# Projections over pairs of 256-token blocks, with 512-column matmuls, in a hybrid GLA and SSD encoder

## The chip, the cores and the metric

The kernel runs on one core of a Trainium2 chip. Its time is the device time of one execution in microseconds (us). One execution is profiled; the durations below are from that one, and the times of the runs stand beside it.

## What is computed

One encoder layer over 2048 prompt tokens and 256 sample tokens, model width 1024, all in float32:

```python
u = _rmsnorm(h, norm_g)
proj = u @ w_in            # q, k, v, z_gla, lr, z_ssd, xbc, dt
...
o = (_gla_direction(q, k, v, la[:, :, 0], False)
     + _flip(_gla_direction(_flip(q), _flip(k), _flip(v), _flip(la[:, :, 1]), True)))
o = _rmsnorm(o, gla_onorm_g).reshape(bt, L, GLA_VAL)
o = o * jax.nn.silu(z_gla.astype(f32))
xbc = jax.nn.silu(_centred_dwconv(xbc, conv_w) + conv_b).astype(f32)
...
y = (_ssd_direction(xs, dt[:, :, 0], A[0], bm, cm, False)
     + _flip(_ssd_direction(_flip(xs), _flip(dt[:, :, 1]), A[1], _flip(bm), _flip(cm), True)))
y = y + d_skip.astype(f32).reshape(SSD_GROUPS, SSD_HPG)[..., None] * xs
y = _rmsnorm(y.reshape(bt, L, SSD_WIDTH) * jax.nn.silu(z_ssd.astype(f32)), ssd_norm_g)
h = h + jnp.concatenate([o, y], axis=-1) @ w_out
h = h + jax.nn.sigmoid(h @ w_ple_gate) * _rmsnorm(p @ w_ple_proj, ple_norm_g)
```

GLA (gated linear attention, 4 heads) and SSD (Mamba-2, 4 groups) are chunked scans, once forward and once backward over the tokens.

## The kernel before

Tokens lie in 9 blocks of 256 (8 of the prompt, 1 of the sample). Each float32 factor of a large product is split into a high and a low part, and the product is three matmuls: high by high (L183), high by low (L184), low by high (L185), made in `mm3`. A projection of one block to 256 columns, a *group*, is so 8 x 2 x 3 = 48 matmuls with 256 streamed columns.

Eight passes go over the blocks, s0 to s7: the even ones a GLA head (blocks 0 to 8), the odd ones an SSD group (blocks 8 to 0). In a pass each block has three groups: `pq` and `pv` (q/k and v) or `pxa` and `pxb` (x, and B with C), and `pz`, the gate of the pass before. Split inputs u are read from DRAM (`uD`, `load_u`) for every block again, in four pieces, two of them early (`Operand`) and two when the third group begins (`rest`).

The first direction of a block (`gla_first`, `ssd_first`) is put into `queue` and is emitted behind a later group by `behind`, up to QMAX behind. The second direction (`second`) needs all blocks of the pass, so it is done in the next pass, behind the group after its gate (`carry`). Until then its running sum y1 and the decayed q (or C), qd, stay in SBUF, 10 buffers each, and only the chunk states U go to DRAM (`put_U`). A GLA block needs its decay first: `gla_decay` makes log decays (`log_decay`: a small matmul into the tile pg, then ScalarE and POOL), cumulative sums on VectorE (L450) and two exponentials, and `gla_qk` multiplies q and k by them while reading PSUM. An SSD block needs a convolution (`ssd_conv`, L604 on VectorE), a B/C product that VectorE masks (cbm, L648) and decay matrices (G, L686 and L687).

After the passes `output` makes three sweeps over the blocks with the output weights (foa, fob, fpg).

A scheduler of the framework orders the instructions of each engine from the program's order and its own cost model. PSUM has 8 banks: 4 with the tag pj (groups and pg), 3 with p1, 1 with p2. All DMAs are issued in one order from SP's queue, and one that waits holds back those behind it.

## Time and profile before

| | |
|---|---|
| time, median of 3 runs | 2574.34 us (2572.82 to 2578.37) |
| the profiled execution | 2581.07 us, its span 2579.3 us |
| TensorE's mean granted clock | 0.974 of full speed |
| TensorE busy | 2437.3 us, 94% |
| VectorE busy | 1744.1 us, 68% |
| ScalarE busy | 1227.3 us, 48% |
| POOL busy | 630.9 us, 24% |
| data moved by SP's queue | 411.66 MB |

Busy times come from one execution; a share is a mean over the whole span. In the trace the first sweep goes to 241 us, the seven later passes to 1756 us, foa to 2037, fob to 2270, and fpg to the end. Tile names are those of the program: `s3b1fpb` is pass 3, block 1, first direction, tile pb; `s4b1d...` is the decay of pass 4's block 1; `pq`, `pv`, `pz`, `pxa` and `pxb` are groups. PE is TensorE, DVE VectorE, ACT ScalarE.

### The profile page before, as it was taken

The page shows a single profiled execution, that of the slowest core. Times are in us where ns is not written, and L with a number is a line of the kernel's source. Part 1 is how long each engine was busy: PE and PEld are TensorE (multiplying, and loading weights), DVE is VectorE, ACT ScalarE, POOL GpSimd, SP SyncE. Part 2 cuts the span into 40 slices and gives each one's busy share as a digit, 9 for nine tenths or more (in the row PEclk, how much of TensorE's full clock was granted, in tenths as well). Part 3 has the DMA queues.
Part 4 walks back from the last instruction along what each step waited for, and adds up shares of the span by engine and source line. Part 5 has one row for each costly group of instructions (what it writes and reads, how often), then busy time and mean ns, then how long its engine had stood idle before and what let it go on. Part 6 is the DMA issues. An engine that isn't in the chain of part 4 may idle for free. (4 is left out here: it accounts for less than half of the span.)

```text
span 2579.3 us, 51675 instructions
## 1 busy us (share of the span) xinstructions
PE 2437.3 (94%) x19736; PEld 2377.1 (92%) x19736; DVE 1744.1 (68%) x4012; ACT 1227.3 (48%) x2468; POOL 630.9 (24%) x649
## 2 busy tenths in 40 slices
PE   7999999899999989999989999998989999998897
PEld 7999999799999979999989999997988889998897
DVE  8886799864579984468997456899623333456665
ACT  5565456644445654445565443565311222355555
POOL 3231000043200023320003330001434432255552
PEclk9999999899999989999999999998999999999998
DMA  6456456544755644465564446555755565512221
GB/s 234 162 173 200 145 184 202 155 138 146 216 169 175 194 135 157 158 201 168 170 206 142 145 150 193 169 162 176 226 163 169 188 207 173 157 51 72 74 75 59
DMA packets 296170, 415.06 MB, mean 161 GB/s; under 512 B 33596, under 2 KB 140904, under 8 KB 295912
## 3 DMA queue, kind: packets, MB, share of 16 engines
q1 hardware_dynamic: 295912, 411.66, 50.7%
q8 instruction: 157, 2.57, 0.4%
q14 instruction: 101, 0.83, 0.1%
HBM read 319.21 MB, written 92.35 MB: 160 GB/s over the span
## 5 line engine op out<-in xcount | busy, mean ns | idle before, releaser
L183 PE MATMUL pz<-u_h,wh_n 128*128 128x256 f32 x896 | 255.6, 285 | 0.0
L185 PE MATMUL pz<-u_h,wl_n 128*128 128x256 f32 x896 | 255.3, 285 | 0.0
L184 PE MATMUL pz<-u_l,wh_n 128*128 128x256 f32 x896 | 255.1, 285 | 0.0
L184 PEld LDWEIGHTS pz<-u_l,wh_n 128*128 128x128 f32 x896 | 171.0, 191 | 0.7 <-issue 0.7
L185 PEld LDWEIGHTS pz<-u_h,wl_n 128*128 128x128 f32 x896 | 170.9, 191 | 0.6 <-issue 0.5
L183 PEld LDWEIGHTS pz<-u_h,wh_n 128*128 128x128 f32 x896 | 171.0, 191 | 0.2
L183 PE MATMUL pxb<-u_h,wh_n 128*128 128x256 f32 x512 | 147.5, 288 | 0.0
L184 PE MATMUL pxa<-u_l,wh_n 128*128 128x256 f32 x512 | 147.2, 287 | 0.0
L183 PE MATMUL pxa<-u_h,wh_n 128*128 128x256 f32 x512 | 146.8, 287 | 0.0
L184 PE MATMUL pxb<-u_l,wh_n 128*128 128x256 f32 x512 | 146.2, 286 | 0.0
L185 PE MATMUL pxb<-u_h,wl_n 128*128 128x256 f32 x512 | 145.8, 285 | 0.0
L185 PE MATMUL pxa<-u_h,wl_n 128*128 128x256 f32 x512 | 145.3, 284 | 0.0
L183 PE MATMUL pq<-u_h,wh_n 128*128 128x256 f32 x384 | 113.4, 295 | 1.6 <-DMA u_h<-uD 1.2
L183 PE MATMUL pv<-wh_n,u_h 128*128 128x256 f32 x384 | 110.9, 289 | 0.7 <-DVE s4b1dm L508 0.2
L185 PE MATMUL pv<-wh_n,u_l 128*128 128x256 f32 x384 | 111.5, 290 | 0.0
L185 PE MATMUL pq<-u_h,wl_n 128*128 128x256 f32 x384 | 111.4, 290 | 0.0
L184 PE MATMUL pq<-u_l,wh_n 128*128 128x256 f32 x384 | 111.2, 290 | 0.0
L184 PE MATMUL pv<-wl_n,u_h 128*128 128x256 f32 x384 | 108.7, 283 | 0.0
L183 PEld LDWEIGHTS pxa<-u_h,wh_n 128*128 128x128 f32 x512 | 97.9, 191 | 1.6 <-issue 1.4
L183 PEld LDWEIGHTS pxb<-u_h,wh_n 128*128 128x128 f32 x512 | 97.9, 191 | 0.7 <-issue 0.7
L184 PEld LDWEIGHTS pxa<-u_l,wh_n 128*128 128x128 f32 x512 | 97.9, 191 | 0.5 <-issue 0.2
L184 PEld LDWEIGHTS pxb<-u_l,wh_n 128*128 128x128 f32 x512 | 97.8, 191 | 0.5 <-issue 0.5
(5981 smaller groups left out, 9561.1 us busy)
## 6 DMA issues: line engine op xcount, KB each, us to landing
u_h<-uD SPq DMA_DIRECT2D x224, 256.0 KB
u_l<-uD SPq DMA_DIRECT2D x224, 256.0 KB
wr_n<-wsec SPq DMA_DIRECT2D x48, 512.0 KB
fx<-xT SPq DMA_DIRECT2D x36, 256.0 KB
h1D<-fx SPq DMA_DIRECT2D x36, 256.0 KB
fh<-h1D SPq DMA_DIRECT2D x36, 256.0 KB
hD<-fh SPq DMA_DIRECT2D x36, 256.0 KB
wr_oa<-wlast SPq DMA_DIRECT2D x8, 512.0 KB
```

The costliest lines, as they stand in the source:

```text
L183: te.matmul(outs, lhsT=lh, rhs=rh, start=start and k == ks[0], stop=False, skip_group_check=True)
L184: te.matmul(outs, lhsT=lh, rhs=rl, start=False, stop=False, skip_group_check=True)
L185: te.matmul(outs, lhsT=ll, rhs=rh, start=False, stop=stop and k == ks[-1], skip_group_check=True)
```

## The change

The seven later passes go over pairs of blocks, `SBS = [(0, 1), (2, 3), (4, 5), (6, 7), (8,)]`, with the last block alone. `proj_pair` makes a group for both blocks of a pair: where tokens are streamed (q/k, x, B/C, z) a matmul has 512 columns, and where tokens are the weights (v) it keeps 256. The 72 pair groups with 512 columns are 28 gates, 28 first groups and 16 SSD second ones, 48 matmuls each. The four pj banks become two tiles of two banks (`bank_pair`); the first sweep and the output sweeps use halves of them. A group is emitted in two halves, with `carried` and `behind` after each. u lies in DRAM by pairs and is loaded in eight pieces (high and low part each 256 KB) with nine buffers each, one piece ahead and seven in `rest`. y1 and qd of every block but a pass's last now go to DRAM too (`keep`) and come back with U in `second_loads`; this makes room in SBUF, and fewer buffers of y1, qd and mx are kept. Raw weights come in quarters. The tile pg of `log_decay` moves from pj to p1.

```diff
 QMAX = 2
+UW = 2 * T
 UK = 2
-UBUFS = 6
+RAWS = 3
+UBUFS = 9
...
+    banks = {"p1": 3, "p2": 1}
+    halves = []
+
+    def bank_pair(name):
+
+        return pp.tile([P, 2, 512], F32, name=name, tag="pj", bufs=2)

     def bank(tag, shape, name):
-        return pp.tile(shape, F32, name=name, tag=tag, bufs=banks[tag])
-
-
-
-    uD = [dram.tile([KT // UK, 2, P, UK, T], F32, name=f"uD{b}") for b in range(NB)]
+        if tag != "pj":
+            return pp.tile(shape, F32, name=name, tag=tag, bufs=banks[tag])
+        if not halves:
+            t = bank_pair(name)
+            halves.extend((t[:, 1], t[:, 0]))
+        h = halves.pop()
+        return h[:, 0:shape[1]] if len(shape) == 2 else h.rearrange("p (f t) -> p f t", f=shape[1])
...
+    uD = [dram.tile([KT, 2, P, T * len(sb)], F32, name=f"uD{n}") for n, sb in enumerate(SBS)]
...
+    yD = [[dram.tile([P, 2, T], F32, name=f"yD{b}_{q}") for q in range(2)] for b in range(NB)]
+    qD = [[dram.tile([P, T], F32, name=f"qD{b}_{q}") for q in range(2)] for b in range(NB)]
...
-    def load_raw(src, tag, kh):
-        raw = upool.tile([P, 4, T], F32, name=f"wr_{tag}_{kh}", tag="uraw", bufs=2)
-        sy.dma_start(raw, src[kh])
+    def load_raw(src, tag, n):
+        raw = upool.tile([P, 2, T], F32, name=f"wr_{tag}_{n}", tag="uraw", bufs=RAWS)
+        sy.dma_start(raw, src[n // 2, :, 2 * (n % 2):2 * (n % 2) + 2])
         return raw
...
+    def proj_pair(w, u, nb, name, token_major):
+        ps = bank_pair(name)
+        flat = ps.rearrange("p f t -> p (f t)").rearrange("p (c t) -> p c t", c=4)
+        def half(h):
+            for k in range(h * KT // 2, (h + 1) * KT // 2):
+                wk, uk = [t[:, k % 4] for t in w[k // 4]], [t[:, 0] for t in u[k]]
+                if token_major:
+                    for c in range(2 * nb):
+                        mm3(flat[:, c], lambda _: [t[:, c * C:(c + 1) * C] for t in uk], lambda _: wk, [k],
+                            k == 0 and c % 2 == 0, k == KT - 1)
+                else:
+                    for f in range(2):
+                        mm3(ps[:, f, :nb * T], lambda _: [t[:, f * P:(f + 1) * P] for t in wk],
+                            lambda _: [t[:, :nb * T] for t in uk], [k], k == 0, k == KT - 1)
+        part = lambda j: flat[:, 2 * j:2 * j + 2] if token_major else ps[:, :, j * T:(j + 1) * T]
+        return half, part
...
-        bufs = {"t4k": 2, "dk": 6, "tm": 2, "zo": 4, "eb": 2, "mx": 7, "q1": 3, "lr": 2, "y1": 10, "qd": 10, "ac": 12,
-                "Us": 1, "Ul": 2, "S1": 2, "S2": 2, "xr": 2, "xc": 2, "ad": 3, "wg": 1, "tot": 3, "hl": 1}
+        bufs = {"t4k": 2, "dk": 6, "tm": 2, "zo": 4, "eb": 2, "mx": 6, "q1": 3, "lr": 2, "y1": 4, "qd": 5, "ac": 12,
+                "yl": 2, "ql": 2, "Us": 1, "Ul": 2, "S1": 2, "S2": 2, "xr": 5, "xc": 2, "ad": 3, "wg": 1, "tot": 3, "hl": 1}
...
-            pg = bank("pj", [P, 2, T], nm + "pg")
+            pg = bank("p1", [P, 2, T], nm + "pg")
...
+        def keep(s, b, U):

             if b == s.order[-1]:
                 s.U = U
             else:
                 sy.dma_start(UD[b][s.i % 2], U)
+                sy.dma_start(yD[b][s.i % 2], s.y1.pop(b).rearrange("p c f i -> p (c f i)").rearrange("p (f t) -> p f t", f=2))
+                sy.dma_start(qD[b][s.i % 2], s.qd.pop(b))
             s.done.add(b)
...
+            if b == s.order[-1]:
+                U, y1, q = s.U, s.y1.pop(b), s.qd.pop(b)
+            else:
+                U, y1, q = tmp("Ul", [P, 2, T], nm + "U"), tmp("yl", [P, 2, 2, C], nm + "y"), tmp("ql", [P, T], nm + "q")
                 sy.dma_start(U, UD[b][s.i % 2])
-            return U, ebc(1 - s.d1, s.h, b, nm + "e2") if s.kind == "s" else None
+                sy.dma_start(q, qD[b][s.i % 2])
+                sy.dma_start(y1.rearrange("p c f i -> p (c f i)").rearrange("p (f t) -> p f t", f=2), yD[b][s.i % 2])
+            return U, y1, q, ebc(1 - s.d1, s.h, b, nm + "e2") if s.kind == "s" else None
...
+            sbs = list(dict.fromkeys(sb_of(b) for b in s.order))
+            for n, sb in enumerate(sbs):
+                last = n == len(sbs) - 1
+                blocks = [b for b in s.order if b in SBS[sb]]
+                if not last:
+                    u2 = load_u(sbs[n + 1], f"u{i}_{sbs[n + 1]}")
                 elif nxt is not None:
+                    u2 = load_u(sb_of(nxt.order[0]), f"u{i}n")
                 else:
                     u2 = gla_mix(NB - 1, "fa8")
+                steps = need(i) if n == 0 else need(i)[1:] + need(i)[:1]
                 for g, (wn, what) in enumerate(steps):
+                    w = get_w(wn)
+                    if g == 2:
                         u2.rest()
+                    half, part_of = proj_pair(w, u, len(blocks), f"p{what}{i}_{sb}", s.kind == "g" and what == "b")
+                    for h in range(2):
+                        late = len(queue)
+                        half(h)
+                        carried()
+                        if s.kind == "g" and what == "a" and h == 0:
+                            for b in blocks[1:]:
+                                gla_decay(s, b, wg, lrs.pop(0))
+                        if h == 0:
                             behind(late)
+                    for b in blocks:
+                        ps = part_of(b - SBS[sb][0])
+                        if what == "z":
+                            zz = gate_z(ps, f"z{i}_{b}")
+                            carry.append(lambda a=(prev, b, zz): second(*a))
+                        elif s.kind == "g" and what == "a":
+                            gla_qk(s, b, ps)
+                        elif s.kind == "g":
+                            v = tmp("mx", [P, 2, T], f"v{i}_{b}")
+                            sc.activation(v, ps, AF.Copy)
+                            hl = [tmp("xr", [P, 2, T], f"v{i}_{b}s{q}", F32R) for q in range(2)]
+                            split(v, *hl, sc, ve)
+                            queue.append(lambda a=(s, b, v, tuple(hl)): gla_first(*a))
                         else:
+                            ssd_raw(s, b, 0 if what == "a" else 1, ps)
+                    behind(late)
+                    if g == 1 and s.kind == "g" and not last:
+                        ahead = [b for b in s.order if sb_of(b) == sbs[n + 1]]
+                        lrs = [load_lr(b, f"s{i}b{b}lr") for b in ahead]
+                        gla_decay(s, ahead[0], wg, lrs.pop(0))
                     elif g == 0 and s.kind == "s" and last and nxt:
+                        ahead = [b for b in nxt.order if sb_of(b) == sb_of(nxt.order[0])]
+                        lrs = [load_lr(b, f"s{i + 1}b{b}lr") for b in ahead]
+                        gla_decay(nxt, ahead[0], wg, lrs.pop(0))
```

The order of instructions shows three places. First TensorE, where pass 3 (SSD) ends and pass 4 (GLA) begins, before the change. Each row is the first of a run for that tile (`pq4_1` is block 1's group in pass 4; s3b1fpb and s3b0fpb are the B/C products of the last two SSD blocks, fpy a product with the decay matrices, s4b1dpg the decay matmul of block 1):

```order
L183 MATMUL pz4_0_12015<-u3n_h0_11574,wh_n11_0_10536 128x256
...
L183 MATMUL pq4_0_12090<-u3n_h0_11574,wh_n12_0_11734 128x256
...
L477 MATMUL s4b1dpg_12193<-s4b1lr_11709,s4wg_10554 128x256
...
L183 MATMUL pv4_0_12219<-wh_n13_0_11869,u3n_h0_11574 128x256
...
L183 MATMUL pq4_1_12352<-u4_1_h0_12003,wh_n12_0_11734 128x256
...
L641 MATMUL s3b1fpb_11935<-s3b1qd_11659,s3b1c0xc_11675 128x128 x2
...
L183 MATMUL pv4_1_12494<-wh_n13_0_11869,u4_1_h0_12003 128x256
...
L183 MATMUL pz4_1_12602<-u4_1_h0_12003,wh_n11_0_10536 128x256
...
L641 MATMUL s3b0fpb_12272<-s3b0qd_11680,s3b0c0xc_11696 128x128 x2
...
L183 MATMUL pq4_2_12684<-u4_2_h0_12340,wh_n12_0_11734 128x256
...
L708 MATMUL s3b0fpy_12401<-s3b0fG1_12306,s3b0fxt_12284 64x128 x4
...
L183 MATMUL pv4_2_12808<-wh_n13_0_11869,u4_2_h0_12340 128x256
```

After the change (`pa4_0` is q/k of blocks 0 and 1 together, `pb4_0` their v, `pa4_1` q/k of blocks 2 and 3):

```order
L203 MATMUL pz4_0_10821<-u3n_h0_10088,wh_n11_0_9512 128x512
...
L203 MATMUL pa4_0_10928<-u3n_h0_10088,wh_n12_0_10310 128x512
...
L679 MATMUL s3b2fpb_10542<-s3b2qd_10211,s3b2c0xc_10227 128x128 x2
...
L679 MATMUL s3b1fpb_10737<-s3b1qd_10237,s3b1c0xc_10253 128x128 x2
...
L203 MATMUL pb4_0_11269<-wh_n13_0_10608,u3n_h0_10088 128x256
...
L679 MATMUL s3b0fpb_10993<-s3b0qd_10258,s3b0c0xc_10274 128x128 x2
...
L746 MATMUL s3b0fpy_11059<-s3b0fG1_11027,s3b0fxt_11005 64x128 x4
...
L517 MATMUL s4b1dpg_11123<-s4b1lr_10287,s4wg_9540 128x256
...
L568 MATMUL s4b0fpa_11442<-s4b0qq1_11201,s4b0dm_10291 128x128
...
L203 MATMUL pa4_1_11396<-u4_1_h0_10803,wh_n12_0_10310 128x512
```

What moved: before, the groups pz4_0 to pq4_2, seven of them, stand ahead of SSD block 0's fpy product, and block 1's decay matmul stands far ahead of it. After, three pairs (pz4_0, pa4_0, pb4_0) do, and the decay matmul of block 1 stands behind it and ahead of pa4_1.

The same place on VectorE, before, behind SSD block 0's masked product (L450 and L452 are the cumulative sums of a decay, fmin a running minimum, ac copies of chunk decays):

```order
L506 SCALAR_TENSOR_TENSOR s4b1qq1_12464<-pq4_1_12352,s4b1dE_12211 128x256
L686 SCALAR_TENSOR_TENSOR s3b0fG1_12306<-s3b0fcbm_12282,s3b0ftm_12286,s3b0fG1_12306 128x128
L450 SCALAR_TENSOR_TENSOR s4b2de_12578<-s4b2dm_12579,bounds_220 128x128
L452 SCALAR_TENSOR_TENSOR s4b2de_12578<-s4b2dm_12579,bounds_220 128x128
...
L686 SCALAR_TENSOR_TENSOR s3b0fG1_12306<-s3b0fcbm_12282,s3b0ftm_12286,s3b0fG1_12306 128x128 x3
L491 TENSOR_TENSOR fmin_223<-fmin_223,s4b2de_12578 128x2
L515 COPY s4b2ac_12761<-s4b2dE_12595 128x1
...
L687 TENSOR_TENSOR s3b0fG1_12306<-s3b0fG1_12306,s3b0ffb1_12295 128x512
...
L506 SCALAR_TENSOR_TENSOR s4b2qq1_12762<-pq4_2_12684,s4b2dE_12595 128x256
...
L687 TENSOR_TENSOR s3b0fG0_12327<-s3b0fG0_12327,s3b0ffb0_12316 128x512
```

After the change, from the same decay matrix G1 on:

```order
L724 SCALAR_TENSOR_TENSOR s3b0fG1_11027<-s3b0fcbm_11003,s3b0ftm_11007,s3b0fG1_11027 128x128 x4
L724 SCALAR_TENSOR_TENSOR s3b0fG0_11048<-s3b0fcbm_11003,s3b0ftm_11007,s3b0fG0_11048 128x128 x4
L725 TENSOR_TENSOR s3b0fG1_11027<-s3b0fG1_11027,s3b0ffb1_11016 128x512
...
L725 TENSOR_TENSOR s3b0fG0_11048<-s3b0fG0_11048,s3b0ffb0_11037 128x512
...
L760 TENSOR_TENSOR s3b0y1_10257<-s3b0fpy_11059,s3b0y1_10257 128x512
L519 TENSOR_SCALAR s4b1dm_11125<-s4b1dpg_11123,bg_279 128x256
L817 TENSOR_TENSOR s3b0lo_11109<-s3b0lpf_11108,s3b0le2_11096 128x2x128
L519 TENSOR_SCALAR s4b1dm_11125<-s4b1dpg_11123,bg_279 128x256
L817 TENSOR_TENSOR s3b1lo_11178<-s3b1lpf_11177,s3b1le2_11105 128x2x128
L490 SCALAR_TENSOR_TENSOR s4b1de_11124<-s4b1dm_11125,bounds_252 128x128
```

What moved: the sums of the decays of s4's blocks 1 and 2 no longer stand among pass 3's last decay matrices; those of block 1 (s4b1dm, L519) stand behind the last sums of SSD block 0.

Last SP's queue, the u loads for block 6 in pass 4 before, with what each waits for:

```order
L176 DMA u4_6_h0_13536<-uD6_75 128x512 [waits DMAHW5_49,PE_49]
L176 DMA u4_6_l0_13537<-uD6_75 128x512 [waits DMAHW6_49]
L176 DMA u4_6_l1_13539<-uD6_75 128x512 [waits DMAHW7_49,PE_49]
L176 DMA u4_6_h1_13538<-uD6_75 128x512 [waits DMAHW0_49,PE_49]
L740 DMA s3b6lU_13881<-UD6_1_172 128x512 [waits DMAHW1_49,Pool_49]
L731 DMA UD4_0_167<-s4b4fU_13640 128x512 [waits DMAHW2_49,Activation_49]
L627 DMA s3b6le2_13883<-ebD6_111 64x2x256 [waits DMAHW3_49,DVE_49]
L627 DMA s3b6le2_13883<-ebD6_111 64x2x256 [waits DMAHW4_49]
L782 DMA mixD4_118<-z4_4zz_13503 128x512 [waits DMAHW5_49,Pool_49]
L787 DMA sqD4_136<-s3b4lo_13603 128x256 [waits DMAHW6_49,Pool_49]
L176 DMA u4_6_l2_13541<-uD6_75 128x512 [waits DMAHW7_49,PE_49]
L176 DMA u4_6_h2_13540<-uD6_75 128x512 [waits DMAHW0_49,PE_49]
```

And those of pair 3 (blocks 6 and 7) after the change:

```order
L196 DMA u4_3_l0_11850<-uD3_72 128x512 [waits DMAHW0_49,PE_49]
L196 DMA u4_3_h0_11849<-uD3_72 128x512 [waits DMAHW1_49,PE_49]
L770 DMA UD2_0_195<-s4b2fU_11816 128x512 [waits DMAHW2_49,Activation_49]
L771 DMA yD2_0_159<-s4b2y1_11482 128x512 [waits DMAHW3_49,Activation_49]
L783 DMA s3b4lq_11985<-qD4_1_182 128x256 [waits DMAHW4_49,PE_49]
...
L826 DMA mixD2_112<-z4_2zz_11809 128x512 [waits DMAHW0_49,Pool_49]
...
L771 DMA yD3_0_161<-s4b3y1_11498 128x512 [waits DMAHW0_49,Activation_49]
...
L831 DMA sqD3_131<-s3b3lo_11993 128x256 [waits DMAHW5_49,Pool_49]
L196 DMA u4_3_l1_11852<-uD3_72 128x512 [waits DMAHW6_49,PE_49]
L196 DMA u4_3_h1_11851<-uD3_72 128x512 [waits DMAHW7_49,PE_49]
L196 DMA u4_3_l2_11854<-uD3_72 128x512 [waits DMAHW0_49,PE_49]
L196 DMA u4_3_h2_11853<-uD3_72 128x512 [waits DMAHW1_49,PE_49]
```

What moved: between the first loads and the rest stood six other transfers, and now stand some twenty; an eighth of the data (two transfers of sixteen) comes early, where half of it did, and the others wait for TensorE one by one.

## Rows read from the trace of the kernel before

**Rows 1.** Page, part 1: busy time, share of the span and count by engine

```profile
span 2579.3 us, 51675 instructions
PE 2437.3 (94%) x19736; PEld 2377.1 (92%) x19736; DVE 1744.1 (68%) x4012; ACT 1227.3 (48%) x2468; POOL 630.9 (24%) x649
```

**Rows 2.** Windows over one SSD and GLA cycle; first row names the columns

```profile
core 0: us, PE busy (x) PEld busy (x) DVE busy (x) ACT busy (x) POOL busy (x), PEclk, DMA share, GB/s
772.00:953.00 181.00, 170.22 (x1364) 161.62 (x1362) 165.12 (x450) 107.39 (x247) 4.99 (x5) 0.96 0.55 173
953.00:1125.00 172.00, 170.55 (x1441) 169.58 (x1442) 94.65 (x206) 75.09 (x121) 66.00 (x86) 1.00 0.50 163
```

**Rows 3.** Timeline of TensorE in a group: start us, us, engine, line, tiles

```profile
600.38 0.28 PE L183 MATMUL pv<-wh_n,u_h 128*128 128x256 f32 x1
...
601.10 0.28 PE L183 MATMUL pv<-wh_n,u_h 128*128 128x256 f32 x1
```

**Rows 4.** Timeline of TensorE, weights of 128 and 64 columns in turn

```profile
97.96 0.28 PE L332 MATMUL g3ps<-p3u_h,wsm 128*128 128x256 f32 x1
98.07 0.28 PE L334 MATMUL g3ps<-p3u_l,wsm 128*64 128x256 f32 x1
...
98.66 0.28 PE L332 MATMUL g3ps<-p3u_h,wsm 128*128 128x256 f32 x1
```

**Rows 5.** Timeline of TensorE, a run of four plain float32 matmuls

```profile
721.64 1.02 PE L705 MATMUL s3b8fpu<-s3b8fxh,s3b8fbt 128*128 128x256 f32 x4
```

**Rows 6.** Timeline of VectorE: a convolution, first mask, last decay matrix

```profile
734.76 1.40 DVE L604 SCALAR_TENSOR_TENSOR s3b7c0cc<-xr,cw,s3b7c0cc 128x256 f32<-128x256 f32 x3
...
778.68 0.68 DVE L648 TENSOR_TENSOR s3b6fcbm<-s3b6fpb,mask 128x512 f32<-128x512 f32 x1
...
953.84 0.74 DVE L687 TENSOR_TENSOR s3b0fG<-s3b0fG,s3b0ffb 128x512 f32<-128x512 f32 x1
```

**Rows 7.** Timeline of TensorE: the bounds of the stretches

```profile
689.92 0.36 PE L183 MATMUL pxa<-u2n_h,wh_n 128*128 128x256 f32 x1
...
957.51 0.38 PE L183 MATMUL pv<-wh_n,u_h 128*128 128x256 f32 x1 [0.15 <-DVE s4b1dm L508]
...
1124.66 0.36 PE L183 MATMUL pxa<-u4n_h,wh_n 128*128 128x256 f32 x1
```

**Rows 8.** VectorE's prices: timeline rows, and a group by line (count, busy, mean ns)

```profile
930.20 0.42 DVE L450 TENSOR_TENSOR_SCAN s4b1de<-s4b1dm,bounds 128x128 f32<-128x128 f32 x1 [1.19 <-POOL s4b1dm L482]
...
933.15 0.48 DVE L479 TENSOR_SCALAR s4b2dm<-s4b2dpg,bg 128x256 f32<-128x256 f32 x1 [0.26 <-ACT s4b2de L478]
...
945.34 0.42 DVE L506 SCALAR_TENSOR_TENSOR s4b1qq<-pq,s4b1dE 128x256 f32<-128x256 f32 x1
...
948.06 0.15 DVE L515 COPY s4b2ac<-s4b2dE 128x1 f32<-128x1 f32 x1
...
956.78 0.67 DVE L508 TENSOR_TENSOR s4b1dm<-pq,s4b1dm 128x512 f32<-128x512 f32 x1
...
958.58 2.87 DVE L513 TENSOR_SCALAR s4b1qkh<-s4b1dm,s4b1dE 128x128 f32<-128x128 f32 x4
...
L147 DVE TENSOR_TENSOR wl_n<-wr_n,wh_n 128x1024 fp32r<-128x1024 f32 x46 | 56.7, 1235 | 26.5 <-ACT wh_n L144 26.3
```

**Rows 9.** Timeline of a decay: its matmul, ScalarE, then POOL

```profile
998.37 0.29 PE L477 MATMUL s4b4dpg<-s4b4lr,s4wg 96*128 96x256 f32 x1
...
1001.15 0.63 ACT L481 ACTIVATE s4b4de<-s4b4de 128x512 f32<-128x512 f32 x1
...
1001.86 1.30 POOL L482 TENSOR_TENSOR s4b4dm<-s4b4dm,s4b4de 128x512 f32<-128x512 f32 x1 [8.70 <-ACT s4b4de L481]
```

**Rows 10.** A window with a burst of transfers, columns as above

```profile
1046.00:1050.00 4.00, 4.00 (x37) 4.00 (x36) 0.43 (x1) 3.96 (x5) 1.30 (x1) 1.00 0.98 344
```

**Rows 11.** Waits of SP's queue: us in total, times, longest us

```profile
SPq L176 <- PE pz L185: 192.3, 164, 4.3
...
SPq L740 <- POOL s5b6lS L443: 8.9, 1, 8.9
```

More of the change, by code (lines that the diff above doesn't have):

```diff
@@ L167, in rest @@
             if self.piece:
-                for n in range(2, KT // UK):
+                for n in range(self.ahead, len(self.parts)):
                     self.piece(n, *self.parts[n])
@@ L388, in prep_dt2, with carried @@
             sy.dma_start(tmD[b], tm)
[L392 to L397 removed]
+        queue, carry, summed, sums_due = [], [], set(), []
+        def carried(ps=None):
+            if carry:
+                carry.pop(0)()
             return ps
         def behind(n):
[L402 removed]
+            if n and queue:
                 queue.pop(0)()
@@ L826, in gla_rstd @@
         def gla_rstd(bs, nm):
+            assert all((b, h) in summed for b in bs for h in range(NH))
             rc = tmp("lr", [NH * len(bs), T], nm + "rc")
@@ L866, in hybrid @@
+        for i, s in enumerate(secs[1:], 1):
+            prev, nxt = secs[i - 1], secs[i + 1] if i < 7 else None
             for n, _ in need(i):
                 get_w(n)
-            for n, b in enumerate(s.order):
-                last = n == NB - 1
-                if i == 0 and b == 0:
-                    pass
-                elif i == 0 and not last:
-                    sums = prep_sums(b + 1, xs)
-                elif not last:
-                    b2 = s.order[n + 1]
-                    if s.kind == "g" and n + 2 < NB:
-                        lrs.append(load_lr(s.order[n + 2], f"s{i}b{s.order[n + 2]}lr"))
-                    u2 = load_u(b2, f"u{i}_{b2}")
+            sbs = list(dict.fromkeys(sb_of(b) for b in s.order))
[4 more added lines that the diff above has]
+                    u2 = load_u(sbs[n + 1], f"u{i}_{sbs[n + 1]}")
@@ L880, in hybrid @@
                 elif nxt is not None:
-                    u2 = load_u(nxt.order[0], f"u{i}n")
+                    u2 = load_u(sb_of(nxt.order[0]), f"u{i}n")
                 else:
                     u2 = gla_mix(NB - 1, "fa8")
-                steps = need(i) if n == 0 or i == 0 else need(i)[1:] + need(i)[:1]
+                steps = need(i) if n == 0 else need(i)[1:] + need(i)[:1]
                 for g, (wn, what) in enumerate(steps):
-                    w, late = get_w(wn), len(queue)
-                    if g == 2 and (i or last):
+                    w = get_w(wn)
+                    if g == 2:
```

225 lines of the change are left out of this document (110 added, 115 removed).

## The prediction, made before the changed kernel was run

> **What bounds the kernel now.** I read the page's busy shares first. TensorE is busy 94% of a span of 2579.3 us and VectorE 68% [rows 1], so a change that makes matmuls cheaper looks as if it were worth its full saving. But a mean hides stages, and the windows by stage show two [rows 2]. One SSD pass and the GLA pass behind it (s3 and s4) make up 435 us, and three such cycles follow each other. In the second half of the SSD pass and the start of the GLA pass (772 to 953 us) VectorE is busy 165.12 of 181 us, while TensorE's granted clock falls to 0.96: TensorE waits there. From 953 us on it is the other way round: VectorE 94.65 of 172 us, TensorE 170.55 at clock 1.00. So the cycle is a VectorE stretch, up to the decay matrices of SSD block 0 (953.84 + 0.74 = 954.6 us [rows 6]), and then a TensorE stretch, from the value projection of block 2 (957.51) to the first matmul of the next SSD pass (1124.66) [rows 7]. The reader is to see that a saving on TensorE counts in full only in the second stretch, and that the first stretch gets shorter only if VectorE starts earlier or has less to do.
>
> **Price of a wide matmul.** A 256-column matmul in a row of its kind follows the one before after 120 ns: six steps in 0.72 us [rows 3]. Where weights of 128 and of 64 columns alternate it is 0.70 / 6 = 117 ns [rows 4]. At 2.4 GHz and one column a cycle, 256 columns would be 106.7 ns, so 13.3 ns come on top with 128 weight columns and 10.0 with a mean of 96: the extra goes with the weights, not with the streamed columns. A 512-column matmul should therefore take 213.3 + 13.3 = 226.7 ns, which I take, and the pair saves 13.3 ns. The bounds: four plain fp32 matmuls over 256 columns took 1.02 us with some 0.38 us of the last one's latency in it, (1.02 - 0.38) / 3 = 213, or 216 ns with rounding [rows 5]; that is 512 cycles at 2.4 GHz or a little over, so they are the nearest row to 512 columns. Twice 120 is 240 ns. The 3,456 wide matmuls (72 groups of 48) would save 46 us if all lay on the path. They don't.
>
> The Trainium skill's page "TensorE: Matmul & The Clock Gate" (section "Back-to-back issue gap") gives N / 2.4 + 2.5 ns for an isolated matmul: 216 at 512 columns, 109 at 256. The second figure disagrees with the 120 ns of this trace, and by the page alone a pair would save only 3 ns, an estimate of 9 us over all wide matmuls.
>
> **The VectorE stretch.** It begins for s3 with its first matmul at 689.92 us [rows 7]. In the new order, block 6's B/C product, which VectorE masks at 778.68 before [rows 6], stands behind two groups of the lone block (48 x 0.12 = 5.8 us each), six wide groups (48 x 0.2267 = 10.9 us each), 15 matmuls of a seventh (3.4 us) and small ones that I put at 6.2 us: 86.6 us, so the mask comes at 776.5, 2.1 us sooner. From there to block 0's last decay matrix I count VectorE's instructions in both orders. Out of the stretch go s4's own (8 scans and 2 drains of 0.42, 4 clamps of 0.48, a split of 0.67, 4 products of 2.87 / 4 = 0.72, a dozen copies and minima of 0.1 to 0.15 [rows 8]: 11.3 us), because only block 0 of s4, not blocks 1 and 2, stands ahead of the last SSD block; and 17 of s3's own steps, mostly convolution steps at 1.40 / 3 = 0.47 [rows 6], which are done before the mask (7.6 us at a mean of 0.45). Into it come 2.5 us of s2's second directions and gates, and 0.9 us for splitting weights in 12 pieces of 0.69 instead of 6 of 1.235 [rows 8], less 0.3 us of edge copies. The balance is -15.8 us of work, at the stretch's busy share 165.12 / 181 = 0.91 [rows 2] -17.4 us of time. Its end moves to 954.6 - 2.1 - 17.4 = 935.1 us. Bounds: nothing at all, if the operations that leave were filling gaps, and -20 us.
>
> **What is paid for that.** The GLA groups that used to cover the end of the VectorE stretch were seven; now six equivalents (three pairs) are issued, and the seventh, the q/k pair of blocks 2 and 3 (pa4_1), stands behind the decay matmul of block 1, which itself stands behind block 0's SSD product. It cannot start sooner for lack of PSUM: one of the two bank pairs holds block 1's q and k until they have been multiplied by their decay, and the other holds the values of pb4_0. From the decay matmul at 998.37 to the end of POOL's 1.30 us at 1003.16 it took 4.8 us [rows 9]; then come 4 scans (1.7 us) and the drains (two of 0.42 and one of 0.67, 1.5 us [rows 8]), and between them two exponentials of 0.63 [rows 9]: 9.3, taken as 9 us, and TensorE has little else in that time. So the TensorE stretch starts at 935.1 + 0.5 (last product) + 9 = 944.6 us instead of 957.5. The bounds of this wait are 0 (block 1's decay is done in the shadow of block 0's last steps) and 9.3 us.
>
> **The TensorE stretch.** Before it is 167.2 us [rows 7]: 21 groups of 5.76 make 121.0, and 46.2 are small matmuls and waits, which I leave. After it holds 288 wide matmuls (65.3 us) and 480 of 256 columns (57.6 us), 122.9 + 46.2 = 169.1 us: one group more. It ends at 1113.7, 11.0 us before 1124.66.
>
> **The sum.** Three cycles give -33 us. The last SSD pass hands over to the output sweep, with no decay to wait for: -2.1 from the mask and -7.6 / 0.91 = -8.4 from the steps done earlier, of which I count -8 in all, since the output sweep waits for transfers of its own as well. Everything else I put at nothing: the first sweep keeps its 256-column matmuls, and its stores in shorter runs, the halved weight loads and the 393 KB that 64 blocks now write to DRAM and read back (64 x 0.393 x 2 = 50 MB) go through queues that moved 163 to 173 GB/s [rows 2] where 344 GB/s were reached [rows 10]; that is the cover, and where it fails is the slow rival below. 2581.07 - 41 = 2540 for the profiled execution, which was 6.7 us above the median of its runs, so 2574.3 - 41 = **2533 us**.
>
> **The token loads.** They are the cover that could break. Each piece now waits for the piece that it overwrites, and seven of eight are issued in the third group of the pair before. Each k is a piece of two times 256 KB: at 344 GB/s [rows 10] 1.5 us, against 1.36 us of matmuls on it. The last of the seven lands some 14 us after that group starts, and is read at about 23.5: a slack of 9.5 us. Between the first and the second piece the queue now holds some twenty other transfers, of which those that store s4's results wait for ScalarE, VectorE and POOL. The longest wait that the queue had on such a store or load was 8.9 us, its longest on TensorE's release of a piece 4.3 us, 192.3 us in 164 times [rows 11].
>
> **The rivals.**
> - Dearer matmuls: 240 ns. The mask comes 4.0 us later and the TensorE stretch is 288 x 0.0133 = 3.8 us longer: 7.8 per cycle, 27 in all with the last pass, **2560 us**. For it speaks only that nothing streamed 512 fp32r columns before; against it, the row with 64 weight columns.
> - Cheaper matmuls, and a warmer clock: at 216 ns the two stretches gain 3.2 and 3.1 us, 22 in all, **2511 us**. For it: the plain fp32 row [rows 5]. The Trainium skill's page "TensorE: Matmul & The Clock Gate" gives the same 216 ns at 512 columns. If TensorE also stops waiting, the 0.04 of clock that is missing over 181 us [rows 2] is worth up to 7 us per cycle: **2490 us**.
> - Slower, the lookahead: if VectorE's end stays at 954.6, the 9.5 us of the decay and the longer TensorE stretch (1.9 us), less the 2.9 that lay between 954.6 and 957.5, cost 8.5 us per cycle: **2599 us**. It decides where the VectorE stretch shortens by less than 8.5 of my 19.5 us. For it: one group less of cover, and block 1's decay behind the last SSD product. Against it: the counted operations, on an engine that is 91% busy.
> - Slower, the loads: a wait of 8.9 us on a store ahead of the pieces, with 4.3 behind it, passes the slack by 3.7 us; at 35 pair starts that is 130 us, **2660 us**. It decides at 41 / 35 = 1.2 us per pair. Against it: such a wait occurred once.
> - No change: the two ends of the VectorE stretch's bounds cancel the rest, **2574 us**.
>
> **How the numbers follow.** The forecast, a gain of 20 to 60 us with 226.7 or so per wide matmul, has 48%; the cheaper matmul with or without the clock 13%; the dearer one or a gain under 20 us 12%; no change 5%; the lookahead 13%; the loads 9%. A measurement of this kernel can tell 0.2% (5 us) from nothing. Faster is 48 + 13 + 12 = 0.73, same 0.05, slower 0.22. The range leaves out the late loads and the far end of the gains: 2490 to 2600 us. The forecast's own is 2514 to 2554.
>
> **What the profile after would show.** Consecutive 512-column matmuls 227 ns apart; 213 to 216 or 240 name the first two rivals. VectorE nearly never idle in the SSD pass, and block 0's last decay matrix done 245 us behind the pass's first matmul, instead of 954.6 - 689.9 = 265. A gap on TensorE ahead of pa4_1 that ends on s4b1's exponentials, some 9 us long: without it that term is wrong, and with it and VectorE's end unmoved it is the lookahead rival. TensorE's waits on transfers of uD at the start of pairs near nothing; several us each are the load rival. A cycle, first matmul of one SSD pass to that of the next, of 424 us instead of 435. The forecast is wrong at its root if VectorE is not what ends the SSD pass once blocks come in pairs.

## The result, and the profile after

The changed kernel takes 2709.94 us (median of 4 runs, 2703.92 to 2716.99) against 2574.2: the ratio is 1.053, with an interval of 1.051 to 1.055. It was forecast at 2533, with a range that ended at 2600. The profiled execution took 2709.12 us. Its page, part 1:

```profile
span 2707.5 us, 45656 instructions
PE 2451.8 (91%) x16280; PEld 2231.1 (82%) x16280; DVE 1752.4 (65%) x4084; ACT 1236.7 (46%) x2542; POOL 629.1 (23%) x651
```

There are 3,456 matmuls fewer, as planned, and yet TensorE's busy time is a little longer than in [rows 1]; its mean granted clock is 0.953 in this execution, where it was 0.974. The first question is where the 128 us of span arose. The first matmuls of pass 1's x group, of foa and of fpg cut both traces into four stages; this table gives their lengths in us, here with the kernels that the experiments below turn on:

| kernel | first sweep | seven passes | foa, fob | last sweep |
|---|---|---|---|---|
| before | 246.9 | 1509.3 | 513.8 | 309.4 |
| after | 283.0 | 1564.4 | 514.4 | 345.7 |
| e1, before with pg in p1 | 254.2 | 1520.5 | 509.9 | 305.6 |
| e2, before with bank pairs | 269.9 | 1565.6 | 515.3 | 313.8 |
| e9, after with single banks, pg in pj | 258.1 | 1536.9 | 510.7 | 289.7 |
| e15, e9 without pairs of blocks | 259.7 | 1542.7 | 501.7 | 290.2 |
| e17, before with DRAM trip, new last-sweep tiles | 246.0 | 1509.7 | 515.0 | 289.3 |

The table compares profiled executions. That of the kernel before took 2581.07 us, 6.7 above its median, so the differences of stages add up to 1 to 18 us less than the ratios of the experiments give.

So 36 us were lost in the first sweep, 55 in the passes and 36 in the last sweep. I had put both sweeps at nothing. In the passes the three cycles are 11.0, 21.4 and 24.5 us longer; the following is the second, s3 and s4. TensorE's timeline first gives the pace of wide matmuls in a group:

```profile
823.77 0.39 PE L203 MATMUL pz<-u_h,wh_n 128*128 128x512 f32 x1
...
827.85 0.39 PE L203 MATMUL pz<-u_h,wh_n 128*128 128x512 f32 x1
```

Eighteen steps in 4.08 us are 226.7 ns, the value I took. Then the places of [rows 6, 7] in the new trace: TensorE's first matmul of s3, the first matmuls of pb4_0 and pa4_1, and that of s5, with VectorE's mask of s3's block 6 and its last decay matrix of block 0.

```profile
737.14 0.28 PE L203 MATMUL pa<-u2n_h,wh_n 128*128 128x256 f32 x1
...
836.92 0.69 DVE L686 TENSOR_TENSOR s3b6fcbm<-s3b6fpb,mask 128x512 f32<-128x512 f32 x1 [2.12 <-PE s3b6fpb L684]
...
978.95 0.78 PE L203 MATMUL pb<-wh_n,u3n_h 128*128 128x256 f32 x1
...
1002.16 0.69 DVE L725 TENSOR_TENSOR s3b0fG<-s3b0fG,s3b0ffb 128x512 f32<-128x512 f32 x1
...
1021.97 0.80 PE L203 MATMUL pa<-u_h,wh_n 128*128 128x512 f32 x1
...
1193.26 0.28 PE L203 MATMUL pa<-u4n_h,wh_n 128*128 128x256 f32 x1
```

From 737.14 to the end of the last decay matrix at 1002.85 it is 265.7 us, where it was 264.7 before and 245 were forecast. The mask of block 6 comes 99.8 us behind the first matmul (88.8 before, 86.6 forecast), and from it to the end of that decay matrix it is 165.9 us (175.9 before, 158.5 forecast). From the end of the decay matrix to pa4_1 it is 19.1 us (2.9 to the next group before, 9.5 forecast), and from pa4_1 to the next SSD pass 171.3 (167.2; 169.1). The cycle takes 456.1 us instead of 434.7; I had forecast 424. The windows of the new trace over the VectorE stretch, over its end, and over the TensorE stretch, with the columns of [rows 2]:

```profile
737.10:1002.80 265.70, 240.73 (x1300) 201.49 (x1298) 224.03 (x586) 136.33 (x333) 5.89 (x13) 0.95 0.63 206
937.20:1022.00 84.80, 57.01 (x324) 46.91 (x322) 69.33 (x188) 38.93 (x96) 9.80 (x14) 0.82 0.50 160
1022.00:1193.00 171.00, 171.00 (x1170) 158.47 (x1171) 88.34 (x211) 76.19 (x128) 58.45 (x72) 0.99 0.51 168
```

and of the kernel before over the same stretches:

```profile
689.90:954.60 264.70, 253.39 (x2053) 242.58 (x2052) 228.29 (x612) 147.13 (x342) 8.87 (x14) 0.97 0.57 176
886.00:957.50 71.50, 59.53 (x447) 54.22 (x445) 62.72 (x177) 42.49 (x88) 7.98 (x7) 0.90 0.46 141
```

VectorE has only 4.3 us less to do in its stretch (228.29, then 224.03), not 15.8, and idles 41.7 instead of 36.4 us. At the end, six GLA groups were issued in 71.5 us before; now four equivalents (pa4_0 and pb4_0) stand in 84.8 us, TensorE is busy 57 of them, and its granted clock falls to 0.82. Ahead of pb4_0, which starts at 979, ScalarE's timeline shows two late reads. The gate group pz4_0 ends at 930 us. Its two gates (z_0zz, z_1zz) are read out of PSUM 42 and 45 us later, behind the last step of s2's block 1 (s2b1lo):

```profile
969.74 0.36 ACT L837 ACTIVATE s2b1lo<-s2b1lpf 1x256 f32<-1x256 f32 x1
...
972.04 0.59 ACT L851 ACTIVATE z_0zz<-pz 128x512 f32<-128x512 f32 x1
...
975.56 0.60 ACT L851 ACTIVATE z_1zz<-pz 128x512 f32<-128x512 f32 x1 [1.15 <-DVE z_0zz L852]
```

and pb4_0 follows the second of them, 49 us behind the end of the gate group. And the decay of block 1, which holds pa4_1, on TensorE and VectorE:

```profile
1007.87 0.58 PE L517 MATMUL s4b1dpg<-s4b1lr,s4wg 96*128 96x256 f32 x1
...
1009.96 0.28 PE L517 MATMUL s4b1dpg<-s4b1lr,s4wg 96*128 96x256 f32 x1
...
1021.23 0.68 DVE L548 TENSOR_TENSOR s4b1dm<-pa,s4b1dm 128x512 f32<-128x512 f32 x1
```

It starts 5 us behind the last decay matrix, because the products of block 0 run ahead of it at the lower of the clock's two levels (1.2 GHz, granted clock 0.50 from 1002 to 1008 us; eight fpy matmuls take 1.12 us there and 0.66 at full clock, at 985 us), and takes 14.0 us to the multiplied k (1021.23 + 0.68), where I had put 9. As long as the two gates hold one bank pair and the q/k group the other, there is no place for a further group. That points to PSUM, which the experiments test.

### The profile page after: what moved, and what is told of

The parts are those of the page before. It is cut to its first block, busy times and chain, and to the rows that moved or that the text cites. A ratio compares the mean times of both kernels' runs of the same rounds, so it can differ in the third digit from the quotient of the medians.

```text
span 2707.5 us, 45656 instructions
## 1 busy us (share of the span) xinstructions
PE 2451.8 (91%) x16280; PEld 2231.1 (82%) x16280; DVE 1752.4 (65%) x4084; ACT 1236.7 (46%) x2542; POOL 629.1 (23%) x651
## 5 line engine op out<-in xcount | busy, mean ns | idle before, releaser
L203 PE MATMUL pa<-u_h,wh_n 128*128 128x512 f32 (+1 forms) x448 | 176.5, 394 | 7.6 <-DVE s6b1dm L548 5.0
L205 PE MATMUL pa<-u_h,wl_n 128*128 128x512 f32 (+1 forms) x448 | 175.3, 391 | 0.0
L204 PE MATMUL pa<-u_l,wh_n 128*128 128x512 f32 (+1 forms) x448 | 172.9, 386 | 0.0
L203 PE MATMUL pz<-u_h,wh_n 128*128 128x512 f32 (+1 forms) x448 | 172.1, 384 | 0.0
L205 PE MATMUL pz<-u_h,wl_n 128*128 128x512 f32 (+1 forms) x448 | 171.8, 384 | 0.0
L204 PE MATMUL pz<-u_l,wh_n 128*128 128x512 f32 (+1 forms) x448 | 170.9, 381 | 0.0
L205 PE MATMUL pb<-u_h,wl_n 128*128 128x512 f32 x256 | 101.7, 397 | 0.0
L204 PE MATMUL pb<-u_l,wh_n 128*128 128x512 f32 x256 | 101.2, 395 | 0.0
L203 PE MATMUL pb<-u_h,wh_n 128*128 128x512 f32 x256 | 100.9, 394 | 0.0
L205 PE MATMUL pb<-wh_n,u_l 128*128 128x256 f32 x336 | 96.0, 286 | 0.0
```

Source lines behind the costliest of these rows:

```text
L203: te.matmul(outs, lhsT=lh, rhs=rh, start=start and k == ks[0], stop=False, skip_group_check=True)
L204: te.matmul(outs, lhsT=lh, rhs=rl, start=False, stop=False, skip_group_check=True)
L205: te.matmul(outs, lhsT=ll, rhs=rh, start=False, stop=stop and k == ks[-1], skip_group_check=True)
```

## The experiments

Each run's ratio is to runs of the kernel before on the same chip; "us" multiplies it by 2574.

**PSUM and the DRAM trip, one at a time on the kernel before.** e1:

```diff
-            pg = bank("pj", [P, 2, T], nm + "pg")
+            pg = bank("p1", [P, 2, T], nm + "pg")
```

> The kernel before, with one edit: the decay tile pg of log_decay comes from the three p1 banks instead of the four pj banks. The changed kernel lost 36 us up to the first matmul of pass 1 (283.0 against 246.9 us), about 57 us over the three passes from SSD to GLA and back, and about 37 us in the last sweep. Theory P (PSUM: fewer independent places, either because pg now competes with the first-direction products in p1, or because pj banks come and go in pairs): this edit alone costs 10 to 40 us, in the first sweep and where GLA passes begin. Theory Q (the DRAM round trip of y1 and qd holds up SP's queue) and theory W (pairs leave too few groups to cover the last SSD blocks): no change, 2574 within 5 us.

Ratio 1.009 (1.006 to 1.012), 23 us. Between the profiled executions it is 7 in the first sweep and 11 in the passes, less 8 in the output sweeps. e2:

```diff
-        return pp.tile(shape, F32, name=name, tag=tag, bufs=banks[tag])
+        if tag != "pj":
+            return pp.tile(shape, F32, name=name, tag=tag, bufs=banks[tag])
+        if not halves:
+            t = pp.tile([P, 2, 512], F32, name=name, tag="pj", bufs=2)
+            halves.extend((t[:, 1], t[:, 0]))
+        h = halves.pop()
```

> The kernel before, with one edit: the four pj banks are handed out as halves of two two-bank tiles, as the changed kernel does, with 256-column groups as before. Theory P: slower by 20 to 70 us, in the first sweep and in the last sweep above all, since a bank comes free only with its twin. Theories Q and W: 2574 within 5 us.

Ratio 1.037 (1.033 to 1.042), 96 us, with no pair of blocks in it: 23 in the first sweep, as in the changed kernel, 56 in the passes, but only 4 in the last sweep, where I had expected much. Theory P holds, at a higher price than expected. The waits of TensorE in e2 (us in total, times, longest) show how:

```profile
PE pz L190 <- DVE z_1zz L812: 7.9, 2, 4.2
PE g5ps L339 <- DVE s0b4dm L486: 4.3, 1, 4.3
```

A matmul that opens a new tile waits until VectorE has read another tile out of PSUM: L812 reads a gate group, L486 the decay tile pg. TensorE's waits on these two lines add up to 37.9 us in e2 and to 0.5 us in the kernel before. e3:

```diff
-        bufs = {... "y1": 10, "qd": 10, ...
+        bufs = {... "y1": 4, "qd": 5, "yl": 2, "ql": 2, ...
...
                 sy.dma_start(UD[b][s.i % 2], U)
+                sy.dma_start(yD[b][s.i % 2], s.y1.pop(b).rearrange("p c f i -> p (c f i)").rearrange("p (f t) -> p f t", f=2))
+                sy.dma_start(qD[b][s.i % 2], s.qd.pop(b))
```

> The kernel before, with one edit: y1 and qd of every block but a pass's last go to DRAM and come back with U, with the changed kernel's buffer counts for them (4 and 5, and two each to come back into). Theory Q: slower by 30 to 60 us, with waits of SP's queue of some 10 us on qd in the first sweep, as in the changed kernel (six of 8 to 10 us there). Theories P and W: 2574 within 10 us.

Ratio 1.057 (1.054 to 1.061), which looks as if theory Q had it. But the last sweep alone, which has no such trip, went from 309.4 to 450.1 us, with four y1 buffers for its h tiles; the first sweep took 246.8 and the passes 1502.8, no more than before. So the trip costs nothing in these stages, though SP's queue does wait on qd (e17 repeats this without the loss in the last sweep).

**The wide matmul.** e4, the changed kernel:

```diff
-                        mm3(ps[:, f, :nb * T], lambda _: [t[:, f * P:(f + 1) * P] for t in wk],
-                            lambda _: [t[:, :nb * T] for t in uk], [k], k == 0, k == KT - 1)
+                        for j in range(nb):
+                            mm3(ps[:, f, j * T:(j + 1) * T], lambda _: [t[:, f * P:(f + 1) * P] for t in wk],
+                                lambda _: [t[:, j * T:(j + 1) * T] for t in uk], [k], k == 0 and j == 0, k == KT - 1)
```

> The changed kernel, with each 512-column matmul made as two of 256 columns, everything else the same. The trace of the changed kernel shows 227 ns for a wide matmul and 120 for a 256-column one, so the 3,456 wide ones hold 46 us. If they are on the path this takes 2710 + 46 = 2756 us; if the groups lie in stretches where TensorE waits for VectorE, as I argued for the SSD passes, only the part in GLA passes shows, 3 x 288 x 0.0133 = 11 to 15 us, 2723. It also tells what the changed structure costs without its gain.

Ratio 1.064 (1.061 to 1.067) against 1.053: the wide matmuls give 1.0%, 27 us (25 between the profiled spans, 17 of them in the passes, where the wide matmuls stand), of the 46 that they hold.

**Mending one suspect in the changed kernel.** e5 put pg into the p2 bank:

```diff
-            pg = bank("p1", [P, 2, T], nm + "pg")
+            pg = bank("p2", [P, 2, T], nm + "pg")
```

> The changed kernel with the decay tile pg in the one p2 bank instead of the three p1 banks. If it is the p1 banks that hold block 1's decay matmul behind the last SSD block's products, the matmul comes some 6 to 10 us sooner in each of three cycles and in the first sweep another 7 us come back: 2710 - 30 = 2680 us. If pg only ends up behind other tenants (p2 serves the second direction and the norms of the first sweep), 2710 within 10 us, or slower.

Ratio 1.066 (1.061 to 1.070), slower. The first sweep came to 262.9 us (20 better) and the passes to 1608.1 (44 worse): the one p2 bank is the better place for pg in the first sweep and the worse one in the passes. e6 moved the decay of block 1:

```diff
+                    elif g == 2 and s.kind == "s" and last and nxt:
+                        gla_decay(nxt, nxt.order[1], wg, lrs.pop(0))
```

> The changed kernel with block 1's decay of a GLA pass put behind the last gate group of the SSD pass before it, instead of behind the first half of that pass's own q/k group. In the planned order pa4_1 then stands ahead of the last SSD block's products instead of behind them. Theory W (the wait ahead of pa4_1, 19 us from the last decay matrix to its first matmul where the kernel before had 3, is block 1's late decay, and groups are there to fill it): the three cycles lose most of their 11 to 20 us: 2710 - 40 = 2670 us. Rival (VectorE's work is the bound through the whole stretch, and the decay only moves on it): 2700 to 2710.

Ratio 1.057 (1.053 to 1.061): nothing gained, 1559.1 us in the passes. The edit did what it should: in e6's trace pa4_1 starts 4.4 us ahead of the end of the last decay matrix, where it started 19.1 us behind it. But from pa4_1 to the next SSD pass it then takes 191.8 us instead of 171.3, and the cycle 459.0 instead of 456.1. So the wait ahead of pa4_1 is not what sets the time. e7 opened a PSUM pool of single banks for the first sweep, one of pairs for the passes, and one of single banks again for the output sweeps:

```diff
+        if pj[0].single:
+            return pj[0].pool.tile(shape, F32, name=name, tag="pj", bufs=4)
```

> The changed kernel with four single pj banks in the first sweep and in the output sweeps, and the two bank pairs in the seven paired passes only. The kernel before with bank pairs lost 23 us up to pass 1, 4 us in the last sweep. So theory P: the first sweep goes from 283 to about 260 us, the last sweep gets 4 us, 2710 - 27 = 2683. If the first sweep's loss is the wait of SP's queue on qd (10 us, six times) instead, the first sweep stays at 283.

Ratio 1.039 (1.035 to 1.042), 36 us better than the changed kernel. The last sweep came back: 288.3 instead of 345.7 us. The first did not (286.9 us to pass 1); TensorE stands idle for 17.5 of the 50 us around the change of pools there, so e7 does not tell what the first sweep lost. Up to the second change of pools the passes are 53 us longer, and behind it foa and fob 35 us shorter. e8 gave the last sweep's tiles eleven buffers in turn:

```diff
-                self.h = [tmp(("y1", ("yl", "eb")[n // 2])[self.b % 2], [P, 2, T], f"{self.nm}h{n}") for n in range(4)]
+                ring = ["y1"] * 4 + ["yl"] * 2 + ["eb"] * 2 + ["uraw"] * 3
+                place = [ring[(4 * self.b + n) % 11] for n in range(4)]
```

> The changed kernel with the last sweep's h tiles going round eleven buffers (y1, yl, eb, and the raw-weight buffers, which stand empty there) and its split p tiles round eleven, instead of two fixed sets of four. The kernel before has ten of each in turn; with only y1's four and qd's five, and everything else as before, that sweep took 450 us instead of 309. Theory B (buffers): 346 goes back to 310 to 318 us, 2710 - 30 = 2680. If it is the smaller mx pool or the bank pairs, 346 stays.

Ratio 1.052 (1.048 to 1.055), last sweep 344.6 us: theory B falls. With e7, it is the bank pairs from which the last sweep suffers, and more buffers don't help it.

**PSUM as before, pairs of blocks kept.** In e9 a wide group takes two of four single banks:

```diff
+    banks = {"pj": 4, "p1": 3, "p2": 1}
...
-        ps = bank_pair(name)
+        one = token_major or nb == 1
+        ps = [bank("pj", [P, 2, T], f"{name}_{f}") for f in range(nb if one else 2)]
...
-            pg = bank("p1", [P, 2, T], nm + "pg")
+            pg = bank("pj", [P, 2, T], nm + "pg")
```

> The changed kernel with its PSUM as before: four pj banks one by one. A group of a pair takes two of them, one for each 128 output columns (or one for each block, where tokens are the weights), so each comes free alone; gates and copies of a pair read them in two instructions each; pg is back in pj. The 512-column matmuls, the pairs, the DRAM round trip and all buffers stay. Theory P: the first sweep's 36 us and the last sweep's 36 us go, and a part of the 58 us that the three cycles lost: 2710 - 72 - 20 = 2620 us. If instead the buffers or the queue cause the sweeps' losses, 2700.

Ratio 1.011 (1.009 to 1.014), 2603 us: 107 of the 136 us are gone. The profiled spans differ by 112: 25 in the first sweep, 28 in the passes, 4 in foa and fob, 56 in the last sweep, where e9 is even 20 us faster than the kernel before. The windows of the last sweep, before, after and in e9, in this order in three fences:

```profile
2270.00:2580.00 310.00, 271.76 (x2155) 268.82 (x2153) 182.17 (x234) 173.82 (x314) 156.33 (x115) 0.94 0.19 61
```

```profile
2362.00:2708.00 346.00, 288.31 (x2203) 280.09 (x2201) 179.57 (x239) 178.00 (x322) 151.57 (x115) 0.91 0.19 61
```

```profile
2306.00:2596.00 290.00, 265.01 (x2154) 258.73 (x2152) 162.56 (x232) 174.71 (x315) 149.72 (x112) 0.98 0.21 68
```

The same matmuls run at a granted clock of 0.91 with bank pairs and 0.98 without; TensorE's idle time and its clock go together (58 and 25 us idle). e10 and e11 gave zo, the buffers into which gates are read, a fifth one, on the changed kernel and on e9:

```diff
-        bufs = {... "zo": 4, ... "qd": 5, ...
+        bufs = {... "zo": 5, ... "qd": 4, ...
```

> The changed kernel with five zo buffers instead of four and, for the room, four qd buffers instead of five. In its trace the gates of pass 4's first pair (z4_0, z4_1) are read out of PSUM only at 972 us, some 20 us after their group, when the second direction of s2's block 1 has given up a zo buffer; until then their two banks are taken, and pb4_0 starts at 979. Theory Z (zo): the gates come earlier, pb4_0 starts 10 to 20 us sooner in each of three cycles: 2710 - 40 = 2670 us. Rival (VectorE's work is the bound there, whatever is free): 2700 to 2710, or slower by qd.

> Both edits of the two runs before this one together. If PSUM and zo are separate causes their gains add up: 2710 - 92 - 40 = 2578 us, at the kernel before. If they are one wait (the gates hold PSUM because zo is full, or zo only matters while PSUM is in pairs), less than the sum: 2600 to 2620.

Ratios 1.050 (1.047 to 1.054) and 1.013 (1.011 to 1.015): theory Z falls, and a fifth buffer gives nothing that can be told from no change. In e10 the gates come as late as without it, 236.1 us behind the first matmul of s3 (234.9 in the changed kernel, where they come 42 us behind their group and not the 20 of the expectation), so zo is not what holds them. In e9 they are read at once, from 200.5 us on, and yet pb4_0 starts only at 259.3, later than in the changed kernel (241.8). So the late gates alone are not what keeps pb4_0 away; what does so in e9 stays open. e12 added the early decay to e11:

> The run before this one with the early decay of block 1, which alone changed nothing (2721 against 2710). If it changed nothing because PSUM and zo kept the groups behind it away, it now gives another 10 to 30 us, 2550 to 2570, faster than the kernel before. If VectorE's work bounds the stretch, 2578 again.

Ratio 1.011 (1.009 to 1.013): again nothing.

**What is left.** e13 and e14 projected the first pair, and the first two, of each GLA pass block by block:

```diff
+                if len(blocks) == 2 and (n == 0 and s.kind == "g"):
+                    steps = ([(g, *x, blocks[:1], False) for g, x in enumerate(turn if n else need(i))]
+                             + [(g, *x, blocks[1:], True) for g, x in enumerate(turn)])
```

> The run with four single banks (e9, 2599 us), in which the first pair of each GLA pass is projected block by block again (z, q/k, v of block 0, then of block 1, 256 columns), all other groups in pairs. If what is left of the loss (14 us per cycle beyond the kernel before, with a gap ahead of pb4_0) comes from a pair's gates and q/k holding all four banks while the last SSD blocks are still in work, single groups fill that gap again: 2599 - 3 x 12 = 2563, 5 to 10 us faster than the kernel before. If VectorE's own work sets the stretch's end whatever the groups do: 2595 to 2605.

> The same with the first two pairs of each GLA pass block by block. If the fill at the pass's start is the point, the second pair adds little: within 5 us of the run before, less by the wide matmuls given back, 3 x 2 x 48 x 13.3 ns x 3 = 6 us at most. If the whole GLA pass is the worse for pairs, another 10 us gain.

Ratios 1.011 (1.008 to 1.014) and 1.015 (1.013 to 1.017); the product in the expectation of e14 comes to 11.5 us, not 6. My reading of the remaining loss, that a pair keeps the filling groups away, falls with them. e15 took every pair apart (the condition of e13 and e14 is then true for every pair):

> The same with every group of the seven passes block by block, so no 512-column matmul at all; tokens still come in pairs, y1 and qd still go through DRAM. It should come back to the kernel before, 2570, if pairs of blocks are the whole of what is left and DRAM trip and token loads cost nothing. If the token loads (one piece of eight early) cost something it stays at 2590 or above.

Ratio 1.006 (1.005 to 1.008), 16 us above the kernel before and 13 below e9, though the profiled spans of the two differ by only 1 us. So at most 13 of e9's 29 us belong to pairs, net of what their wide matmuls save, which e15 gives up; the first sweep (259.7 us) and the passes (1542.7) lose as much without any. e16 gave groups a fifth bank:

```diff
-    banks = {"pj": 4, "p1": 3, "p2": 1}
+    banks = {"pj": 5, "p1": 2, "p2": 1}
```

> The run with four single banks with a fifth for groups, taken from the first-direction products, which keep two. If the four banks are what a pair runs out of where pass 4 begins, the gap ahead of pb4_0 shrinks and the three cycles gain 5 to 10 us each: 2580. If the products need their three banks it is slower, 2620 or more, since each SSD block's products then queue.

Ratio 1.007 (1.005 to 1.009), whose interval touches that of e9, and spans 2 us apart: no gain of the size expected. But one wait of e9 is gone in e16's trace, that of the q/k pair at the start of a GLA pass on the gate ahead of it:

```profile
PE pa L190 <- DVE z_0zz L843: 15.3, 3, 5.1
```

In e16 pb4_0 starts 21 us sooner behind the first matmul of s3, and the three cycles are 3.5, 5.3 and 4.4 us shorter than in e9. The last SSD pass (8.8 us longer) and the first sweep (4.6) take it back; that the two p1 banks do this is argued, not shown.

**The part that pays.** The changed kernel also gives the last sweep's tiles for h and p other buffers, a part of the change that is not described above. e17 is the kernel before with the DRAM trip and these tiles; e18 adds buffers where SBUF came free.

```diff
-                self.h = [tmp("y1", [P, 2, T], f"{self.nm}h{n}") for n in range(4)]
+                self.h = [tmp(("y1", ("yl", "eb")[n // 2])[self.b % 2], [P, 2, T], f"{self.nm}h{n}") for n in range(4)]
...
-        bufs = {... "dk": 6, ... "zo": 4, ... "mx": 7, ...
+        bufs = {... "dk": 8, ... "zo": 6, ... "mx": 8, ...
```

> The kernel before with the DRAM trip of y1 and qd (as e3) and with the changed kernel's tiles of the last sweep, in which even blocks take y1 and qd and odd ones yl, eb and the state tiles. e3 lost 141 us in the last sweep alone, where only four y1 buffers were left, and gained some 10 us in all other stages together. With the tiles mended the last sweep should take 290 us, as in the single-bank runs, or 310, as before: 2550 to 2570 us, not slower than the kernel before. If the DRAM trip costs anything that e3's last sweep hid, 2580 or more.

> The same, with the SBUF that the DRAM trip frees given to the tiles that the starts of GLA passes run short of: dk 8 instead of 6, zo 6 instead of 4, mx 8 instead of 7. No pairs, 256-column groups. If buffers of decays and gates hold up these starts, 5 to 10 us per cycle: 2530 to 2545 us. If VectorE's work and PSUM set them, the same as the run before this one.

Ratios 0.993 (0.992 to 0.995) and 0.991 (0.989 to 0.993): 2562.5 and 2554.9 us on a chip where the kernel before took 2580.4, so both are faster than both kernels. The window of e17's last sweep, and a wait of its SP queue on qd:

```profile
2271.00:2560.00 289.00, 265.00 (x2153) 258.60 (x2151) 162.55 (x234) 174.01 (x314) 154.76 (x115) 0.99 0.21 68
```

```profile
SPq L735 <- DVE s4b4qd L508: 7.4, 1, 7.4
```

All of e17's gain is in the last sweep (309.4 to 289.3); the first sweep and the passes are where they were, with SP's queue held up for up to 7.4 us at a time. What e18 adds lies in foa and fob (499.7 us), not in the starts of GLA passes (passes 1512.2), for which I had meant it; foa and fob took 501.7 us in e15 too, without these buffers, so that they are the cause is not shown.

## Why the prediction was wrong, step by step

- **Price of a wide matmul: right.** 226.7 ns forecast and measured; e4 puts what it is worth at 27 us of 46. The Trainium skill's page "TensorE: Matmul & The Clock Gate" (section "Back-to-back issue gap") has 216 ns for an isolated matmul of this width; the trace disagrees by 11 ns and decides.
- **Everything else at nothing: this step failed, and carries the most.** It spoke of stores, weight loads and the DRAM trip, and left out two lines of the diff: four banks that become two pairs, which the prediction names only in the wait ahead of pa4_1, and pg among p1's tenants. On the kernel before these cost 96 and 23 us (e2, e1), on the changed one 107 together (e9). They account for 25 of the 36 us in the first sweep and for more than all 36 in the last. The DRAM trip, which I did look at, cost nothing that e17 shows.
- **The VectorE stretch: failed.** The forecast was 19.5 us shorter; it is 1.0 longer. 13.2 us of the miss lie ahead of block 6's mask, where TensorE is the bound (busy 97.2 of 99.8 us). The 304 wide and 95 narrow group matmuls ahead of it, 80.3 us, are as I counted them (303 and 96); small matmuls and waits take 19.5 us where I put 6.2 without a row. The same remainder is 15.1 us in the kernel before (88.8 us, less 614 group matmuls at 0.12). Single banks do not mend this (98.5 us in e9). The other 7.4 us lie behind the mask: that part is 10.0 us shorter, not 17.4. I took the convolutions done before the mask as a gain of time, but they are done in the same stretch: over the whole of it VectorE has 4.3 us less to do and idles 5.3 us more.
- **What is paid at the end: right in kind, mis-sized.** 19.1 us instead of 9.5, ending on block 1's decay as described; I had priced the chain at the full clock, and behind one product only. That the decay itself costs the time is not borne out: e6 and e12 issue it earlier and gain nothing.
- **The TensorE stretch: right,** 171.3 us for 169.1. **The last SSD pass: mis-sized,** 1.9 us shorter up to the output sweep, not 8.
- **The rivals.** The lookahead rival was nearest in kind (2599), and its condition, VectorE's end unmoved, came true. It could not reach 2710, since no rival priced PSUM. The token loads, which I feared most, don't show: no wait of TensorE on uD stands among the waits of the new trace. Some such waits stand in other runs, 6.7 us in all in e9 and 5.1 in e15, where the kernel before has 2.0.

What stays open: the 16 us that e15 keeps without pairs and with PSUM as before. Pair-wise token loads, quarter weights, groups in two halves, the smaller mx and x in five half-size buffers (xr) are common to e9 and e15 and absent from e17; no run took them apart. Nor is it shown why bank pairs cost the last sweep 56 us with the new tiles and 4 with the old ones, or what in these tiles gains 20 us.

## What to carry to other kernels

Price the PSUM of a change before its matmuls: a bank that comes free only with its twin (96 us here), or a small tile moved among busier tenants (23 us), can cost stages that the change does not mean to touch. Do not count a wider matmul's saving in full where TensorE waits for others (27 of 46 us here), and look at the banks that its wider result holds until its slowest reader is done. When one edit bundles several, run the parts alone: here the part that looked dearest, the trip through DRAM, cost nothing, and a new choice of tiles in the last sweep, with the buffers of e18, made the fastest kernel.

## What the hardware showed that I had not expected

TensorE's mean granted clock went with its idle time: 0.98 in the last sweep of e9 and 0.91 in the changed kernel's for nearly the same matmuls (2154 and 2203), and 0.82 over the end of a VectorE stretch in which it was busy 57.0 of 84.8 us. A stall can so cost twice, once as waiting and once as slower matmuls behind it, as the fpy matmuls did (1.12 us for eight, 0.66 at full clock). And SP's queue could stand still for some 7 us on qd, time and again, in a kernel (e17) that lost nothing by it in the passes.
